# Score and value matmuls of a sliding-window attention, issued alternately between two halves of the array

## The chip, the cores and the metric

The kernel runs on one core of a Trainium2 chip, in one launch. The metric is the device time of that launch in microseconds (us), as the median of several runs. PE is the matmul engine, PEld its weight load, DVE, ACT and POOL are the vector, scalar and GpSimd engines, SP is the queue that issues most DMAs.

## The reference, cut to what matters

The program is one inference step of a one-layer hybrid decoder: LayerNorm and adaLN modulation, a combined input projection, a Mamba-2 group and a sliding-window attention group side by side, an output projection, and a squared-ReLU MLP. 2048 prompt tokens and 32 sample tokens go through it. The change touches the prompt's attention alone:

```python
WINDOW = 128; HEAD_DIM = 64; N_Q = 8; N_KV = 2; Q_PER_KV = 4
...
s = jnp.einsum('bnqgrd,bnkgd->bngrqk', qb, kk) * (HEAD_DIM ** -0.5)
s = jnp.where(mask[None, :, None, None], s, -jnp.inf)
p = sink_softmax(s, sinks.astype(jnp.float32).reshape(N_KV, Q_PER_KV)[:, :, None, None])
o = jnp.einsum('bngrqk,bnkgd->bnqgrd', p, vv)
```

A block of 128 queries looks at the keys of its own block and of the one before. A head has 64 elements, so a score contracts over 64 rows, and the values of one key-value head give 64 output columns.

## The kernel before, in words

The work goes through the chip in stages. **Sweep 1** (the functions named `st_...`) takes 16 prompt tiles of 128 tokens and one tile of sample tokens, and makes for each the modulated input, the projection to dt, q, k and v ("slab": `st_slab`, 24 matmuls for each of two halves), and the whole attention. Sweep 2 makes the Mamba group (`xproj`, `zproj`, `ssd1`, `ssd2`), and after it come the output projection and the MLP. Sweep 1 ends some 400 us after the start of the span; the MLP takes most of the rest.

In sweep 1 the loop over `i` handles several tiles at once, each at another step: slab 0 of tile i, `st_PT` of tile i-2, `st_score` of tile i-1, slab 1 of tile i, one step of the adaLN weights (`ada_mm`, L257, four column strips of 32; eight such steps in all), `st_PV` of tile i-2, `st_qkT` of tile i, and the transposes of a later tile's input (L320).

- `st_qkT` (L395) transposes q (L406) and a doubled k (L410: each key head stands twice, in partitions 0 to 63 and 64 to 127). ACT rounds the results to the type fp32r (`qh`, `kTh`), DVE keeps the remainders (`ql`, `kTl`).
- `st_score` (L414) makes the scores of a tile. For each key-value head `g` and each parity `par` of the query head it takes one PSUM buffer and writes two score blocks into it, each by `mm3` (L164): high by high (L165), high by low (L166), low by high (L167). That is 4 buffers and 24 matmuls a tile. `par` chooses the partitions, 0 to 63 or 64 to 127, and by that the rows of the array. ACT (L433) and DVE (L434) copy the buffers out into `S`, and `softmax` (L378) follows: a maximum on DVE, eight exponentials on ACT (L389), a scaling on POOL (L393).
- `st_PT` (L438) transposes the probabilities (L449). `st_PV` (L456) multiplies them with the values: for each of one or two terms, and each `g`, one matmul with 64 output columns at column 0 or 64 of the array (L461), all in plain float32. ACT copies the result to `ao` (L464) and stores it.

The PSUM buffers come from three rings: `mm` with 3 buffers, `tr` with 2, `sc` with 3. A buffer is taken again when its last reader is done.

The order of the instructions on each engine is not the order of the code. The framework's scheduler sorts them, engine by engine, when the program is built, by a model of its own of how long each takes; only what depends on each other, and what is pinned by hand, keeps its order. On the chip each engine then works through its list and waits where a semaphore isn't there yet.

Of the kernel before, what the change touches and what calls it, by code (L numbers as in the profile page):

```python
# [118 lines left out]
def body(tc, I, O):  # L119
    nc = tc.nc  # L120
    V, S, G, PE, D = nc.vector, nc.scalar, nc.gpsimd, nc.tensor, nc.sync
# [14 lines left out]
    def sc_tile():  # L136
        return ps.tile([128, 512], F32, tag="sc", name="sc", bufs=3)
# [18 lines left out]

    def sum2(out, tmp, w):
        PE.matmul(out[:ND, :w], lhsT=idt[:2 * ND, 192:224], rhs=tmp[:2 * ND, :w], start=True, stop=True)

    def split(hi, lo, src, eng=None):  # L160
        S.activation(hi, src, AF.Copy)  # L161
        (eng or V).tensor_tensor(lo, src, hi.bitcast(F32), ALU.subtract)  # L162

    def mm3(out, ahi, alo, bhi, blo, first=True, last=True):  # L164
        PE.matmul(out, lhsT=ahi, rhs=bhi, start=first, stop=False)  # L165
        PE.matmul(out, lhsT=ahi, rhs=blo, start=False, stop=False)  # L166
        PE.matmul(out, lhsT=alo, rhs=bhi, start=False, stop=last)  # L167
# [63 lines left out]
    start = ExitStack()  # L231
# [66 lines left out]
    kTh = p1.tile([128, 2, 3, 128], F32R, name="kTh")  # L298
    kTl = p1.tile([128, 2, 3, 128], F32R, name="kTl")
# [46 lines left out]
    def st_slab(t, n):  # L346
# [8 lines left out]
        if t == NTILE:  # L355
            tmp = mm_dec(p1.tile([128, 512], F32, tag="ao", name="tmp", bufs=2), 388, lambda k: hh[:, 0, k, :2 * ND],
                         lambda k, l: (W1l if l else W1h)[k][:, sl])
            sum2(mm, tmp, 388)
        elif t > 2:
            for k in range(8):  # L360
                mm3(mm[:P, :388], hh[:, 0, k, :P], hh[:, 1, k, :P], W1h[k][:, sl], W1l[k][:, sl], k == 0, k == 7)
# [16 lines left out]
    def softmax(p, Sx, P, nh, nk, sink):  # L378
        mx = p.tile([128, 8], F32, tag="mx", name="mx", bufs=2)
        nm = p.tile([128, 8], F32, tag="nm", name="nm", bufs=2)  # L380
        su = p.tile([128, 8], F32, tag="su", name="su", bufs=2)
        ex = p.tile([128, 8], F32, tag="ex", name="ex", bufs=2)
        V.tensor_reduce(mx[:P, :nh], Sx, AX.X, ALU.max)
        V.scalar_tensor_tensor(mx[:P, :nh], mx[:P, :nh], 0.125, sink, ALU.mult, ALU.max)
        V.tensor_scalar(nm[:P, :nh], mx[:P, :nh], -1.0, None, ALU.mult)
        V.tensor_tensor(ex[:P, :nh], sink, mx[:P, :nh], ALU.subtract)
        S.activation(ex[:P, :nh], ex[:P, :nh], AF.Exp)
        for h in range(nh):
            S.activation(Sx[:, h, :], Sx[:, h, :], AF.Exp, bias=nm[:P, h:h + 1], scale=0.125,  # L389
                         accum_out=su[:P, h:h + 1])  # L390
        V.tensor_tensor(su[:P, :nh], su[:P, :nh], ex[:P, :nh], ALU.add)
        V.reciprocal(su[:P, :nh], su[:P, :nh])
        G.tensor_tensor(Sx, Sx, su[:P, :nh].unsqueeze(2).to_broadcast([P, nh, nk]), ALU.mult)  # L393
# [20 lines left out]
    def st_score(t):  # L414
        qh, ql = tl.pop(("q", t))
        if t == 0:
            slots, nk, ci = slice(0, 1), 1, 0
        else:
            slots, nk, ci = [(slice(0, 3, 2), 2, 0), (slice(0, 2), 2, 1), (slice(1, 3), 2, 1)][t % 3]
        ge = cc(C_GE, 128).bitcast(U32).unsqueeze(1).to_broadcast([128, 2, 128])  # L420
        Sx = p1.tile([128, 8, 128], F32, tag="S", name="S", bufs=2)
        if t == 0:
            V.memset(Sx, NEG)
        for g in range(2):
            for par in range(2):
                sc = sc_tile().rearrange("p (j s n) -> p j s n", j=2, s=2)
                rp = slice(64 * par, 64 * par + 64)
                for jj in range(2):
                    q2 = 2 * g + jj
                    mm3(sc[:, jj, 0:nk, :], qh[rp, q2, :], ql[rp, q2, :], kTh[rp, g, slots, :], kTl[rp, g, slots, :])  # L430
                hs = slice(4 * g + 2 * par, 4 * g + 2 * par + 2)
                if t > 0:
                    S.activation(Sx[:, hs, :], sc[:, :, 1 - ci, :], AF.Copy)  # L433
                V.copy_predicated(Sx[:, hs, :], ge, sc[:, :, ci, :])  # L434
        softmax(p1, Sx, 128, 8, 128, sm[:, 3, :])
        tl["S", t] = Sx
# [19 lines left out]
    def st_PV(t):  # L456
        terms = tl.pop(("PT", t))
        o = sc_tile()
        for i, (vv, pt) in enumerate(terms):
            for g in range(2):  # L460
                PE.matmul(o[64 * g:64 * g + 64, :], lhsT=vv[:, 64 * g:64 * g + 64], rhs=pt[:, g, :],  # L461
                          start=i == 0, stop=i == len(terms) - 1, tile_position=(0, 64 * g))
        ao = p1.tile([128, 4, 128], F32, tag="ao", name="ao", bufs=2)
        S.activation(ao.rearrange("p r n -> p (r n)"), o, AF.Copy)  # L464
        S.dma_start(out=att_d[t], in_=ao)
# [219 lines left out]
    n = len(seq)  # L685
# [66 lines left out]
    for i in range(n + 3):  # L752
        if i == 10:
            start.close()
        g = lambda j: seq[j] if 0 <= j < n else None
# [11 lines left out]
        if g(i - 1) is not None and g(i - 1) < NTILE:  # L767
            st_score(g(i - 1))
# [4 lines left out]
        if g(i - 2) is not None and g(i - 2) < NTILE:  # L773
            st_PV(g(i - 2))
# [568 lines left out]
    def dec_steps():  # L1343
# [12 lines left out]
        for n in range(2):  # L1356
            sum2(pp[n], b[:, 512 * n:512 * n + 512], 512)
# [166 lines left out]
```

## Time and profile before

| | |
|---|---|
| median of 3 runs | 2519.69 us (2519.55 to 2523.37) |
| profiled execution, its own time | 2522.31 us |
| its span, first to last instruction | 2520.5 us |
| granted clock of the matmul engine, mean | 0.985 |
| DVE busy | 1510.5 us (60%) |
| ACT busy | 720.2 us (29%) |
| POOL busy | 930.8 us (37%) |

Two views carry the prediction. One gives the busy time of each engine in stretches of the span. The other lists the instructions of one engine in order of time: start in us, how long the row lasts, engine, line, operation, out<-in, shapes, how many instructions in a row were merged ("x2"), and in brackets what an idle engine waited for. A float32 matmul whose operands aren't of type fp32r stands there as two records. The records of matmuls overlap, so what one costs is read from the starts, not from the lengths.

### The profile page before, as it was taken

What the parts mean: (1) busy time and instruction counts of PE and PEld (TensorE: products, weight loads), DVE (VectorE), ACT (ScalarE), POOL (GpSimd) and SP (SyncE); (2) the same over time, 40 slices, a digit from 0 to 9 for tenths busy, and PEclk for the clock granted to TensorE, in tenths of its full rate; (3) what the DMA queues carried; (4) which work ended last, traced back from release to release, by engine and by line L of the source; (5) the groups of instructions that cost most, each with busy time, mean ns of one, the idle gap of its engine ahead of it and who ended that gap; (6) DMA issues with size and microseconds to landing.
All of it is one profiled execution on the core that took longest, in us unless ns stands there. A gap on an engine that the chain in (4) does not pass through costs nothing.

```text
span 2520.5 us, 32205 instructions
## 1 busy us (share of the span) xinstructions
PE 2421.1 (96%) x12694; PEld 2004.7 (80%) x12694; DVE 1510.5 (60%) x2582; ACT 720.2 (29%) x1434; POOL 930.8 (37%) x602
## 2 busy tenths in 40 slices
PE   7899999999998988899999999999999999999997
PEld 6567787977997766787888888887788988988985
DVE  6756666977788988744434444447844344344347
ACT  3544465333342222222121211213221221221221
POOL 4323431233223544633243333426532332332335
PEclk9999999999999999899999999999999999999998
DMA  8644333223335336411111211118211111111111
GB/s 318 255 173 160 118 124 91 73 72 109 98 115 174 117 127 221 162 59 58 48 59 42 63 51 39 53 43 238 100 51 34 43 59 34 43 59 34 43 46 70
DMA packets 116504, 244.19 MB, mean 97 GB/s; under 512 B 25984, under 2 KB 61248, under 8 KB 113200
## 3 DMA queue, kind: packets, MB, share of 16 engines
q1 hardware_dynamic: 111952, 232.15, 27.6%
q10 hardware_dynamic: 4400, 9.98, 1.1%
q8 instruction: 100, 1.64, 0.3%
q14 instruction: 52, 0.43, 0.1%
HBM read 187.74 MB, written 55.37 MB: 96 GB/s over the span
## 4 chain that ended last, share of the span: by engine, by line
PE 53%; DVE 3%; POOL 1%; issue 1%; DMA 0%; ACT 0%; SPq 0%; POOLq 0%; DVEq 0%; ACTq 0%
PE sc L165 10%; PE sc L167 10%; PE sc L166 10%; PE mm L165 5%; PE mm L167 5%; PE mm L166 5%; PE tr L165 2%; PE tr L167 2%; PE tr L166 2%; PE tr L1276 1%; DVE p L1231 1%; DVE nb L1300 0%; DVE p L1232 0%; POOL rs L173 0%; DVE p L1307 0%
## 5 line engine op out<-in xcount | busy, mean ns | idle before, releaser
L162 POOL TENSOR_TENSOR wdl<-st,wdh 128x1024 fp32r<-128x1024 f32 x63 | 164.1, 2605 | 531.4 <-ACT wdh L161 531.4
L1261 DVE TENSOR_TENSOR r<-r 128x320 f32<-128x320 f32 (+1 forms) x160 | 151.3, 946 | 299.0 <-ACT u L1257 101.6
L1288 DVE TENSOR_TENSOR p<-mm,p 128x512 f32<-128x512 f32 x298 | 202.7, 687 | 176.6 <-PE mm L167 176.6
L161 ACT ACTIVATE wdh<-st 128x1024 fp32r<-128x1024 f32 x63 | 66.8, 1061 | 628.4 <-PE mm L167 245.4
L165 PE MATMUL sc<-H,wvh 128*128 128x352 f32 (+1 forms) x640 | 227.1, 355 | 5.3 <-ACT r L1255 5.3
L167 PE MATMUL sc<-H,wvl 128*128 128x352 f32 (+1 forms) x640 | 226.1, 353 | 0.0
L166 PE MATMUL sc<-H,wvh 128*128 128x352 f32 (+1 forms) x640 | 225.9, 353 | 0.0
L165 PE MATMUL sc<-H,wuh 128*128 128x352 f32 (+1 forms) x640 | 224.4, 351 | 0.0
L167 PE MATMUL sc<-H,wul 128*128 128x352 f32 (+1 forms) x640 | 223.9, 350 | 0.0
L166 PE MATMUL sc<-H,wuh 128*128 128x352 f32 (+1 forms) x640 | 223.6, 349 | 0.0
L1255 ACT ACTIVATE r<-sc 128x352 f32<-128x352 f32 (+1 forms) x160 | 81.7, 511 | 271.6 <-PE sc L167 230.9
L165 PEld LDWEIGHTS sc<-H,wvh 128*128 128x128 f32 x640 | 120.8, 189 | 18.3 <-ACT r L1255 5.7
L166 PEld LDWEIGHTS sc<-H,wvh 128*128 128x128 f32 x640 | 120.7, 189 | 12.0
L167 PEld LDWEIGHTS sc<-H,wvl 128*128 128x128 f32 x640 | 120.4, 188 | 12.1
L165 PEld LDWEIGHTS sc<-H,wuh 128*128 128x128 f32 x640 | 120.4, 188 | 11.4 <-ACT r L1255 0.8
L167 PEld LDWEIGHTS sc<-H,wul 128*128 128x128 f32 x640 | 120.8, 189 | 10.5
L166 PEld LDWEIGHTS sc<-H,wuh 128*128 128x128 f32 x640 | 120.7, 189 | 10.2
L1137 DVE TENSOR_TENSOR st<-st,gf 128x1024 f32<-128x1024 f32 x64 | 83.8, 1309 | 55.6 <-POOL wdl L162 46.3
L1288 DVE TENSOR_TENSOR p<-tr,p 128x512 f32<-128x512 f32 x102 | 69.9, 687 | 74.8 <-PE tr L167 74.8
L173 POOL TENSOR_TENSOR rs<-ve,mhalf 128x1 f32<-128x1 f32 (+2 forms) x68 | 49.1, 722 | 174.9 <-DVE ve L172 158.1
L1260 DVE TENSOR_TENSOR ud<-r 128x32 f32<-128x32 f32 x32 | 56.5, 1766 | 94.4 <-ACT r L1255 94.4
L652 DVE SCALAR_TENSOR_TENSOR xc<-xq,cvw,xc 128x256 f32<-128x256 f32 x192 | 102.0, 535 | 2.7
(485 smaller groups left out, 6630.8 us busy)
## 6 DMA issues: line engine op xcount, KB each, us to landing
st<-in_wd SPq DMA_DIRECT2D x64, 512.0 KB
st<-in_wu SPq DMA_DIRECT2D x63, 512.0 KB
wa<-in_w_ada SPq DMA_DIRECT2D x32, 512.0 KB
hT_d<-hb SPq DMA_DIRECT2D x16, 1024.0 KB
hT<-hT_d SPq DMA_DIRECT2D x16, 512.0 KB
hT<-hT_d SPq DMA_DIRECT2D x8, 1024.0 KB
csb<-cs_d SPq DMA_DIRECT2D x16, 512.0 KB
p<-xhat_d SPq DMA_DIRECT2D x16, 512.0 KB
```

The lines of the kernel that those rows point to most:

```text
L161: S.activation(hi, src, AF.Copy)
L162: (eng or V).tensor_tensor(lo, src, hi.bitcast(F32), ALU.subtract)
L165: PE.matmul(out, lhsT=ahi, rhs=bhi, start=first, stop=False)
L166: PE.matmul(out, lhsT=ahi, rhs=blo, start=False, stop=False)
L167: PE.matmul(out, lhsT=alo, rhs=bhi, start=False, stop=last)
L173: G.tensor_tensor(r[:P], v[:P], mhalf[:P, 0:n], ALU.pow)
L652: V.scalar_tensor_tensor(dst_, src(j), cvw[:, f, j:j + 1], dst_, ALU.mult, ALU.add)
L1137: V.tensor_tensor(st, raw, scale, ALU.mult)
L1255: S.activation(r[:, :n], mm[:, :n], AF.Relu)
L1260: V.tensor_tensor(ud, r[:, w:n], r[:, w:n], ALU.mult)
L1261: V.tensor_tensor(r[:, :w], r[:, :w], r[:, :w], ALU.mult)
L1288: V.tensor_tensor(acc[t][:, sl], mm, acc[t][:, sl], ALU.add)
```

## The change

A helper, `side_by_side`, calls a list of functions that each issue a matmul, and ties each instruction to the one before it by an edge without a semaphore: the scheduler must keep them in this order, and the chip waits for nothing. It may still put other instructions between them.

`st_score` now opens the buffers of both parities of a `g` first and issues their matmuls in turn, parity 1 and then parity 0. The fourth buffer of a tile (`g` = 1, `par` = 1) comes from the `mm` ring. `st_PV` puts its matmuls in the same chain, `g` = 1 before `g` = 0. The copies, the softmax and all other code stay as they were.

```diff
+    def side_by_side(calls):
+        prev = None
+        for fn in calls:
+            ins = fn()
+            if prev is not None:
+                tc.add_manual_dep(ins.ins, prev.ins.name,
+                                  mybir.DependencyInfo(mybir.DependencyClass.NoSync, mybir.DependencyReason.DATA),
+                                  reason="side_by_side")
+            prev = ins
...
+        rp = lambda par: slice(64 * par, 64 * par + 64)
         for g in range(2):
+            scs = [(sc_tile, mm_tile)[g * par]().rearrange("p (j s n) -> p j s n", j=2, s=2) for par in range(2)]
+            side_by_side([lambda jj=jj, i=i, par=par: PE.matmul(
+                scs[par][:, jj, 0:nk, :], lhsT=(ql if i == 2 else qh)[rp(par), 2 * g + jj, :],
+                rhs=(kTl if i == 1 else kTh)[rp(par), g, slots, :], start=i == 0, stop=i == 2)
+                for jj in range(2) for i in range(3) for par in (1, 0)])
             for par in range(2):
-                sc = sc_tile().rearrange("p (j s n) -> p j s n", j=2, s=2)
-                rp = slice(64 * par, 64 * par + 64)
-                for jj in range(2):
-                    q2 = 2 * g + jj
-                    mm3(sc[:, jj, 0:nk, :], qh[rp, q2, :], ql[rp, q2, :], kTh[rp, g, slots, :], kTl[rp, g, slots, :])
+                sc = scs[par]
...
-        for i, (vv, pt) in enumerate(terms):
-            for g in range(2):
-                PE.matmul(o[64 * g:64 * g + 64, :], lhsT=vv[:, 64 * g:64 * g + 64], rhs=pt[:, g, :],
-                          start=i == 0, stop=i == len(terms) - 1, tile_position=(0, 64 * g))
+        side_by_side([lambda i=i, vv=vv, pt=pt, g=g: PE.matmul(
+            o[64 * g:64 * g + 64, :], lhsT=vv[:, 64 * g:64 * g + 64], rhs=pt[:, g, :], start=i == 0,
+            stop=i == len(terms) - 1, tile_position=(0, 64 * g))
+            for i, (vv, pt) in enumerate(terms) for g in (1, 0)])
```

Since the scheduler sorts anew, everything in sweep 1 moves a little; from early in sweep 2 on the lists of all engines are the same. PE has 12117 matmuls before and after. In the changed program the lines of the old code stand ten to twelve higher: L437 is a score matmul, L471 a value matmul, L416 and L420 are the transposes of q and k, L267 is an adaLN matmul.

The first place is on PE, the scores of tile 7, where the numbers tell the PSUM buffers apart. Before, `sc_2207` and `sc_2225` belong to parity 0 and `sc_2216` to parity 1:

```order
L165 MATMUL sc_2207<-kTh_139,qh_2113 128x256
L166 MATMUL sc_2207<-kTl_140,qh_2113 128x256
L167 MATMUL sc_2207<-kTh_139,ql_2114 128x256
L165 MATMUL sc_2207<-kTh_139,qh_2113 128x256
L166 MATMUL sc_2207<-kTl_140,qh_2113 128x256
L167 MATMUL sc_2207<-kTh_139,ql_2114 128x256
L165 MATMUL sc_2216<-kTh_139,qh_2113 128x256
L166 MATMUL sc_2216<-kTl_140,qh_2113 128x256
L167 MATMUL sc_2216<-kTh_139,ql_2114 128x256
L165 MATMUL sc_2216<-kTh_139,qh_2113 128x256
L166 MATMUL sc_2216<-kTl_140,qh_2113 128x256
L167 MATMUL sc_2216<-kTh_139,ql_2114 128x256
```

After it, at the same tile, `sc_2208` is parity 1 and `sc_2207` parity 0 of the first head; `mm_2226` is the fourth buffer:

```order
L437 MATMUL sc_2208<-kTh_139,ql_2114 128x256
L437 MATMUL sc_2207<-kTh_139,ql_2114 128x256
L437 MATMUL sc_2208<-kTh_139,qh_2113 128x256
L437 MATMUL sc_2207<-kTh_139,qh_2113 128x256
L437 MATMUL sc_2208<-kTl_140,qh_2113 128x256
L437 MATMUL sc_2207<-kTl_140,qh_2113 128x256
L437 MATMUL sc_2208<-kTh_139,ql_2114 128x256
L437 MATMUL sc_2207<-kTh_139,ql_2114 128x256
L437 MATMUL mm_2226<-kTl_140,qh_2113 128x256
L437 MATMUL sc_2225<-kTl_140,qh_2113 128x256
L437 MATMUL mm_2226<-kTh_139,ql_2114 128x256
L437 MATMUL sc_2225<-kTh_139,ql_2114 128x256
```

Six matmuls of one parity in a row became a strict alternation, and the fourth buffer's six, which stood in a run of their own 20 rows later, have joined the others.

The second place is on PE too, the value matmuls of one tile. Before, the two matmuls of a term (`PT_1749`) are apart, with four transposes between them; "x2" is one matmul for each column half:

```order
L257 MATMUL mm_1858<-wa_1660,scT_109 32x512
L461 MATMUL sc_1883<-PT_1749,v_1064 64x512
L406 MATMUL tr_1895<-idt_74,qkv_1720 128x128 x4
L461 MATMUL sc_1883<-PT_1749,v_1064 64x512
L461 MATMUL sc_1883<-PC_1750,vd_1751 64x512 x2
L410 MATMUL tr_1902<-idt_74,kd_1891 128x128 x2
```

And with the change:

```order
L267 MATMUL mm_1858<-wa_1658,scT_109 32x512 x2
L267 MATMUL mm_1858<-wa_1660,scT_109 32x512 x2
L471 MATMUL sc_1883<-PT_1749,v_1064 64x512 x2
L471 MATMUL sc_1883<-PC_1750,vd_1751 64x512 x2
L272 MATMUL mm_1869<-part_1867,idt_74 9x512
```

Here the halves stand together, and the adaLN matmuls ahead of them are not broken up any more.

The third place is on PE at the last tile, where the scheduler puts the first four scores of a tile (one for each buffer, high by high) ahead of the rest. Before, 29 rows of `xproj` matmuls stand between the transposes of k (L410) and the first score; the first of them:

```order
L461 MATMUL sc_3829<-PC_3722,vd_3723 64x512
L410 MATMUL tr_3850<-idt_74,kd_3839 128x128 x2
L166 MATMUL mm_4235<-hT2_3856,pg0_3981 128x256
L167 MATMUL mm_4235<-hT2_3855,pg1_3982 128x256
L165 MATMUL mm_4235<-hT2_3855,pg2_3985 128x256
```

And with the change:

```order
L471 MATMUL sc_3829<-PC_3722,vd_3723 64x512 x2
L416 MATMUL tr_3843<-idt_74,qkv_3692 128x128 x4
L420 MATMUL tr_3850<-idt_74,kd_3839 128x128 x2
L437 MATMUL sc_3918<-kTh_139,qh_3841 128x256
L437 MATMUL sc_3917<-kTh_139,qh_3841 128x256
L437 MATMUL mm_3936<-kTh_139,qh_3841 128x256
L437 MATMUL sc_3935<-kTh_139,qh_3841 128x256
L175 MATMUL mm_3999<-hT2_3855,Wx00_3683 128x256
```

The scores that need the copies of these very transposes now follow them at once. The same holds at tiles 0, 1, 8 and 10 to 14, with none or one to three rows between.

On ACT, at the same last tile and with the change, the copies `qh` and `kTh` (L171) stand behind the eight exponentials of the tile before (L399):

```order
L399 ACTIVATE S,su<-S,nm 128x128
L397 ACTIVATE ex<-ex 128x8
L399 ACTIVATE S,su<-S,nm 128x128 x7
L171 ACTIVATE qh<-tr 128x512
L171 ACTIVATE kTh<-tr 128x2x128
L171 ACTIVATE pg_4133<-wzst 128x512
```

Before, the order of these three is the same, but PE had other work in between.

## The prediction

> **What bounds the kernel now.** I read the page first: its busy times and the first line of its chain of waits.
>
> ```profile
> PE 2421.1 (96%) x12694; PEld 2004.7 (80%) x12694; DVE 1510.5 (60%) x2582; ACT 720.2 (29%) x1434; POOL 930.8 (37%) x602
> PE 53%; DVE 3%; POOL 1%; issue 1%; DMA 0%; ACT 0%; SPq 0%; POOLq 0%; DVEq 0%; ACTq 0%
> ```
>
> PE is the engine on which the end waits. But the change works in sweep 1 alone, so the second view is the busy time by stretch, from 100 us to the end of sweep 1. Columns: PE, PEld, DVE, ACT, POOL, then the granted clock.
>
> ```profile
> 100.00:200.00 100.00, 100.00 (x571) 66.76 (x564) 58.82 (x148) 47.09 (x156) 27.52 (x26) 1.00 0.51 177
> 200.00:300.00 100.00, 100.00 (x602) 77.79 (x601) 64.40 (x178) 44.13 (x140) 37.60 (x30) 1.00 0.34 117
> 300.00:320.00 20.00, 13.88 (x69) 8.86 (x67) 13.73 (x19) 8.61 (x16) 11.26 (x6) 0.74 0.76 240
> 340.00:360.00 20.00, 19.53 (x137) 16.84 (x134) 17.80 (x26) 14.05 (x28) 13.12 (x7) 1.00 0.39 139
> 380.00:400.00 20.00, 14.56 (x89) 9.80 (x88) 15.49 (x51) 14.90 (x41) 1.90 (x1) 0.83 0.04 14
> ```
>
> From 100 to 300 us PE has no idle time at all, and no other engine is above 65%. There a us of PE work that goes is a us of the kernel. From 300 us on PE idles now and then; the waits of PE between 60 and 450 us say for whom (total us, times, longest):
>
> ```profile
> PE sc L165 <- DVE S L434: 9.3, 3, 6.1
> PE mm L568 <- DVE dkw L559: 3.0, 1, 3.0
> ```
>
> The 9.3 us are scores that wait until DVE has emptied a score buffer: a tile needs four, the ring has three.
>
> **The change, part by part.** No matmul, copy or DMA is added or removed; what changes is how PE's matmuls lie beside each other. The third view, PE in order of time between 200 and 230 us, prices that.
>
> ```profile
> 200.60 1.03 PE L320 MATMUL tr<-idt,xb 128*128 128x128 f32 x8
> 201.56 0.38 PE L165 MATMUL sc<-kTh,qh 64*128 64x256 f32 x1
> 201.78 0.28 PE L166 MATMUL sc<-kTl,qh 64*128 64x256 f32 x1
> 201.90 0.28 PE L167 MATMUL sc<-kTh,ql 64*128 64x256 f32 x1
> 201.91 0.39 PE L165 MATMUL sc<-kTh,qh 64*128 64x256 f32 x2
> 202.13 0.28 PE L166 MATMUL sc<-kTl,qh 64*128 64x256 f32 x2
> ...
> 202.97 0.28 PE L167 MATMUL sc<-kTh,ql 64*128 64x256 f32 x1
> 203.17 0.44 PE L166 MATMUL mm<-pg,hb 128*128 128x388 f32 x1
> ...
> 206.72 1.90 PE L257 MATMUL mm<-wa,scT 128*32 128x512 f32 x10
> 208.55 0.38 PE L165 MATMUL sc<-kTh,qh 64*128 64x256 f32 x1
> ...
> 209.46 1.06 PE L257 MATMUL mm<-wa,scT 128*32 128x512 f32 x6
> 210.45 1.08 PE L461 MATMUL sc<-PT,v 128*64 128x512 f32 x4
> 211.36 1.03 PE L461 MATMUL sc<-PC,vd 128*64 128x512 f32 x4
> 212.31 0.66 PE L406 MATMUL tr<-idt,qkv 128*128 128x128 f32 x4
> ...
> 217.49 0.50 PE L165 MATMUL sc<-kTh,qh 64*128 64x256 f32 x3
> 217.92 0.84 PE L158 MATMUL mm<-tmp,idt 64*32 64x388 f32 x2
> ...
> 228.64 1.07 PE L461 MATMUL sc<-PT,v 128*64 128x512 f32 x2
> 229.64 0.55 PE L320 MATMUL tr<-idt,x 128*128 128x128 f32 x3
> ```
>
> *Scores.* A score starts 0.12 us after the one before it in the same rows of the array (201.78 and 201.90). Two of different parity start together: the rows "x2" hold one of each. This already happens without the change: the list has six of parity 0, six of parity 1, six of parity 0, and these 18 take 203.17 - 201.56 = 1.61 us, that is 12 slots of 0.116 and 0.2 for going into and out of the narrow shape. The other six of the tile stand alone: 208.55 to 209.46, 0.91 us, six slots and 0.2. The three at 217.49 (parities 0, 1, 0) take 0.43: two slots and 0.2. So a run costs 0.2 + 0.116 per slot, and a tile has 18 slots now and 12 when all pair up. That is 6 x 0.116 x 15 = 10.4 us, and some 0.4 for tile 0, whose matmuls are half as wide. The lists have 48 runs of scores before and 36 with the change: 12 x 0.2 = 2.4 us. Together 13.2 us.
>
> [...]
>
> *Values.* Four records, one matmul for each column half, take 210.45 to 211.36; two such pairs in a row 1.86 us; one matmul alone 228.64 to 229.64 = 1.00 us. So a slot costs 0.87 us, holding one half or both, and a run 0.13 more. Of 31 pairs, 8 cost a slot too many in the list of before (as `PT_1749` above: half alone, then three); with the change all 31 stand together. 8 x 0.87 = 7.0, and 30 runs become 22, 8 x 0.13 = 1.0. Together 8.0 us.
>
> *adaLN matmuls, a side effect.* Eight in one piece take 1.85 us:
>
> ```profile
> 188.99 1.92 PE L257 MATMUL mm<-wa,scT 128*32 128x512 f32 x16
> 190.84 1.08 PE L461 MATMUL sc<-PT,v 128*64 128x512 f32 x4
> ```
>
> Broken by six scores they take 1.83 (206.72 to 208.55) and 0.99 (209.46 to 210.45): 0.97 us more for one more piece. The eight steps lie in 16 pieces before, in 10 after: 6 x 0.97 = 5.8 us.
>
> *Neighbours.* The eight transposes ahead of 201.56 take 0.96 us, about 0.09 more than 8 x 0.109, the step between transposes inside such a row (0.66 us for the four at 212.31 holds three steps and one full length). Runs of the three narrow kinds fall from 94 to 68: 26 x 0.09 = 2.3 us.
>
> PE's work falls by 13.2 + 8.0 + 5.8 + 2.3 = **29.3 us**.
>
> *A wait that goes.* The fourth score buffer comes from the `mm` ring now, so the 9.3 us of waits for L434 go. If DVE is late all the same, the next user of the ring waits; the value lies between 0 and 9.3, and I take 9.3, since the first scores are now issued 3 us and more ahead of most others.
>
> *A wait that comes.* At tiles 0, 1, 8 and 10 to 15 the first scores stand right behind the transposes that feed them. How long the copies take, from the same execution:
>
> ```profile
> 297.08 0.66 PE L406 MATMUL tr<-idt,qkv 128*128 128x128 f32 x4
> 297.83 0.60 ACT L161 ACTIVATE qh<-tr 128x512 fp32r<-128x512 f32 x1 [0.92 <-PE tr L406]
> ...
> 298.92 0.44 PE L410 MATMUL tr<-idt,kd 128*128 128x128 f32 x2
> 299.39 0.39 ACT L161 ACTIVATE kTh<-tr 128x256 fp32r<-128x256 f32 x1 [0.95 <-PE tr L410]
> ```
>
> From L410 to the end of `kTh` 0.86 us pass, of which PE's own two transposes fill 0.2. So at least 0.65 us a tile, 9 x 0.65 = 6 us in all. The other end comes from what stands before these copies on ACT: eight exponentials, and before those DVE's work on the scores (counts, busy us, mean ns):
>
> ```profile
> L389 ACT ACTIVATE S<-S,nm 128x128 f32<-128x128 f32 x128 | 49.6, 390 | 21.1 <-DVE nm L385 21.1
> L434 DVE COPY_PREDICATED S<-c,sc 128x256 f32<-128x256 uint32 x64 | 26.2, 440 | 12.5 <-ACT S L433 12.5
> L389 ACT ACTIVATION_READ_ACCUMULATOR S<-S,nm 128x1 f32 x128 | 24.2, 189 | 0.0
> L383 DVE TENSOR_REDUCE mx<-S 128x8 f32<-128x1024 f32 x16 | 19.5, 1217 | 0.3
> ```
>
> After the last score: 4 x 0.44 + 1.22 + about 1 of small work on DVE, then 8 x (0.39 + 0.19) = 4.6 on ACT, then up to 0.6 (`ao`) + 0.5 (`qkv`) + 0.60 + 0.39: some 10 to 12 us until `kTh` is there. In PE's list some 7 to 9 us of work stand between at tiles 10 to 14, and 3 us at tile 15. That is 1 to 5 us each for five tiles, and up to 9 for the last. At the upper end 5 x 4 + 9 + 2 = 31 us. I take 2 us for tiles 10 to 14, 5 for the last, 2 for the other three: 17 us, nearer the middle, since ACT idles about half of this time now. Behind a waiting score stand the next tile's slab on PE, and behind that everything.
>
> *Nothing else.* POOL (607 instructions) and SP (537) keep theirs, a few rows swap places; ACT loads its tables ten times less (1.28 us each) at the end of sweep 1, where ACT is not the bound; I count nothing.
>
> **Sum.** -29.3 - 9.3 + 17 = -21.6 us. The profiled execution took 2522.31 (span 2520.5 and 1.8 around it), so 2500.7; the median of the runs stands 2.6 lower, and the forecast for a median is 2519.69 - 21.6 = **2498 us**.
>
> **The rivals.**
> *The copies become the bound* (2511). The new waits come out at the upper end, and the 9.3 come back elsewhere: -29.3 + 31 - some 10 for what doesn't add = about -8. For it: the rows of tiles 10 to 15 above. Against: DVE at 64% and ACT at 44% from 200 to 300 us. [...]
> *No new waits* (2484). Only the 6 us at the lower end: -29.3 - 9.3 + 6 = -32.6, and up to 3 more from clock that is not lost (0.74 around the wait at 306 us).
> *The pairs don't form* (2510). If strict alternation went one by one, only values and adaLN would gain: -8.0 - 5.8 + the waits. Against: the three at 217.49 alternate and took two slots.
> *Slower: the `mm` ring* (2545). A score holds one of three `mm` buffers from the first four scores until the copies; slab and adaLN accumulators have two left. If each of two slabs a tile waited 1.5 us behind the exponentials on ACT, 32 x 1.5 = 48 - 21.6 = +26. It decides from 0.7 us a slab. Against: in the list only two slabs follow within 2 us of the score that held their buffer.
>
> **How the numbers follow.** Forecast (2490 to 2506) 0.5; no new waits 0.17; copies as the bound 0.2; no pairs 0.06; slower 0.07. Two in ten may be left out: the slow rival and part of both tails, so the range is 2482 to 2513. A measurement of this kernel tells about 0.2%, 5 us, from no change. Faster by more than that: 0.5 + 0.17 + most of 0.2 and 0.06 = 0.87; within it 0.07; slower 0.06.
>
> **What would show it.** The scores of a tile in 12 starts instead of 18, one run of 20 in about 1.4 us; no value matmul alone, 0.87 us a pair; L257 in 10 pieces; no wait of a score for L434, but waits of a score for ACT's `kTh` at the nine tiles. It would be wrong if slabs wait for ACT's copies of `mm` buffers, if PE's idle time from 200 to 400 us grows by over 30 us, or if the paired starts fall apart.

## The result, and the profile after

| | before | after |
|---|---|---|
| median | 2521.53 us (4 runs) | 2507.18 us (4 runs) |
| profiled execution, its own time | 2522.31 us | 2506.52 us |
| its span | 2520.5 us | 2504.7 us |
| mean granted clock | 0.985 | 0.984 |

The ratio is 0.9941, with a 95% interval of 0.9926 to 0.9956: 14.4 us faster. The kernel was run again later on, beside other runs of the kernel before, and gave 2506.66 us and 0.9946 (0.9933 to 0.9958).

The busy times on the page of the changed kernel, and under them the stretches that were shown of before (columns as there):

```profile
PE 2396.3 (96%) x12694; PEld 1996.7 (80%) x12694; DVE 1501.9 (60%) x2582; ACT 705.1 (28%) x1424; POOL 930.2 (37%) x602
```

```profile
100.00:200.00 100.00, 96.59 (x630) 68.37 (x628) 63.94 (x165) 48.72 (x164) 34.85 (x31) 1.00 0.52 184
200.00:300.00 100.00, 93.31 (x576) 72.23 (x572) 65.34 (x176) 51.25 (x163) 44.06 (x31) 0.98 0.44 148
300.00:320.00 20.00, 19.26 (x115) 15.87 (x114) 9.02 (x23) 9.02 (x31) 6.68 (x6) 0.93 0.49 156
340.00:360.00 20.00, 12.54 (x90) 10.03 (x88) 15.11 (x34) 13.36 (x41) 8.76 (x6) 0.83 0.39 128
380.00:400.00 20.00, 20.00 (x122) 16.68 (x121) 12.56 (x46) 8.98 (x20) 2.09 (x2) 1.00 0.30 102
```

PE lost 24.8 us of busy time over the kernel, but the kernel only 15.8 in these two executions: between 100 and 300 us PE was never idle before, and now is for 10 us. The waits of PE between 60 and 430 us name what it is idle for (total, times, longest):

```profile
PE sc L437 <- ACT kTh L171: 13.0, 9, 4.9
PE tr L330 <- DVE mv L190: 5.6, 1, 5.6
PE tr L416 <- DVE qkv L386: 3.5, 2, 2.5
PE sc L471 <- DVE S L446: 2.8, 1, 2.8
PE mm L272 <- ACT part L270: 2.0, 1, 2.0
```

The waits of scores for DVE's copies (L434 before) are gone; nine first scores wait for `kTh`. PE in order of time shows the pairs. These are 20 of the 24 scores of a tile; "x2" is one score of each parity:

```profile
212.16 0.39 PE L437 MATMUL sc<-kTl,qh 64*128 64x256 f32 x2
212.38 0.28 PE L437 MATMUL sc<-kTh,ql 64*128 64x256 f32 x2
212.50 0.28 PE L437 MATMUL sc<-kTh,qh 64*128 64x256 f32 x2
...
213.34 0.28 PE L437 MATMUL mm<-kTh,ql 64*128 64x256 f32 x1
213.34 0.28 PE L437 MATMUL sc<-kTh,ql 64*128 64x256 f32 x1
213.55 0.39 PE L153 MATMUL mm<-pg,hb 128*64 128x388 f32 x1
```

Ten starts, 0.12 us apart, 1.39 us in all. The values now always stand with both halves together, 0.9 us a pair:

```profile
200.32 1.08 PE L471 MATMUL sc<-PT,v 128*64 128x512 f32 x4
201.23 1.03 PE L471 MATMUL sc<-PC,vd 128*64 128x512 f32 x4
```

**A better yardstick than the total.** All these programs hold the same 12694 matmul records, and the 3000th starts in sweep 2, at 520.5 us before. From there to the 4700th (780 us) the two executions run in step: the lead of the changed kernel is 18.2 us at the 3000th and 18.2 at the 4700th. In the output projection, from 780 to 1030 us, where PE waits for DVE, POOL and inputs on their way, the lead goes down to about 13 and comes out at 15.8; with most other kernels below it goes up there. So I compare kernels by the start of the 3000th record as well, and split it into the time that PE had no matmul running (idle) and the rest (work), counted over the PE records from the 300th, which starts at 54.3 to 54.7 us in all.

| kernel | median us | ratio to before (95%) | 3000th at | idle | work |
|---|---|---|---|---|---|
| before | 2521.53 | | 520.5 | 21.2 | 444.8 |
| the change | 2507.18 | 0.9941 (0.9926 to 0.9956) | 502.3 | 32.7 | 415.2 |
| again | 2506.66 | 0.9946 (0.9933 to 0.9958) | 501.7 | 31.9 | 415.3 |
| scores_only | 2512.82 | 0.9968 (0.9956 to 0.9980) | 509.9 | 32.6 | 423.0 |
| values_only | 2513.41 | 0.9965 (0.9954 to 0.9977) | 508.7 | 21.9 | 432.2 |
| sc4 | 2510.38 | 0.9962 (0.9948 to 0.9976) | 509.1 | 29.7 | 425.1 |
| mm4 | 2511.47 | 0.9962 (0.9949 to 0.9975) | 507.4 | 27.9 | 425.3 |
| parity01 | 2515.15 | 0.9977 (0.9968 to 0.9985) | 511.2 | 32.2 | 424.6 |
| remfirst | 2521.02 | 0.9996 (0.9986 to 1.0006) | 517.4 | 42.0 | 421.0 |
| halves | 2542.33 | 1.0082 (1.0066 to 1.0098) | 539.6 | 38.1 | 447.2 |
| dvecopies | 2510.33 | 0.9955 (0.9940 to 0.9969) | 507.2 | 29.8 | 423.1 |
| dvecopies_rem | 2528.71 | 1.0024 (1.0013 to 1.0034) | 525.9 | 49.1 | 422.4 |
| swap | 2493.48 | 0.9893 (0.9878 to 0.9908) | 493.2 | 22.9 | 416.0 |
| swap_rem | 2493.81 | 0.9892 (0.9879 to 0.9906) | 493.2 | 23.8 | 414.6 |

The change took 29.6 us of work off PE and put 11.5 us of idle time in.

### The profile page after: what moved, and what is told of

The parts are those of the page before. It is cut to its first block, busy times and chain, and to the rows that moved or that the text cites. A ratio compares the mean times of both kernels' runs of the same rounds, so it can differ in the third digit from the quotient of the medians.

```text
span 2504.7 us, 32204 instructions
## 1 busy us (share of the span) xinstructions
PE 2396.3 (96%) x12694; PEld 1996.7 (80%) x12694; DVE 1501.9 (60%) x2582; ACT 705.1 (28%) x1424; POOL 930.2 (37%) x602
## 4 chain that ended last, share of the span: by engine, by line
PE 54%; DVE 3%; POOL 1%; issue 1%; DMA 0%; SPq 0%; ACT 0%; POOLq 0%; DVEq 0%; ACTq 0%
PE sc L175 11%; PE sc L177 10%; PE sc L176 10%; PE mm L175 5%; PE mm L177 5%; PE mm L176 5%; PE tr L177 2%; PE tr L175 2%; PE tr L176 2%; PE tr L1288 1%; DVE p L1243 1%; DVE nb L1312 0%; DVE p L1244 0%; POOL rs L183 0%; DVE p L1319 0%
## 5 line engine op out<-in xcount | busy, mean ns | idle before, releaser
L171 ACT ACTIVATE wdh<-st 128x1024 fp32r<-128x1024 f32 x63 | 66.8, 1061 | 629.0 <-PE mm L177 244.8
L175 PEld LDWEIGHTS sc<-H,wvh 128*128 128x128 f32 x640 | 120.8, 189 | 18.2 <-ACT r L1267 5.6
```

## The experiments

### The parts of the change

**scores_only**: the change, with the value matmuls in the old form.

```diff
-        side_by_side([lambda i=i, vv=vv, pt=pt, g=g: PE.matmul(
-            o[64 * g:64 * g + 64, :], ...
-            for i, (vv, pt) in enumerate(terms) for g in (1, 0)])
+        for i, (vv, pt) in enumerate(terms):
+            for g in range(2):
+                PE.matmul(o[64 * g:64 * g + 64, :], ...
```

> Only the scores alternate (with the fourth buffer from the mm ring); the value matmuls are issued as before. Theory (the terms add: PE time per slot and run, plus waits): the list has 28 runs of value matmuls with 8 extra slots, against 22 runs and none with the whole change, 8 x 0.87 + 6 x 0.13 = +7.8 us, and 32 runs of scores against 36, 4 x 0.3 = -1.2. The first scores stand as close behind the transposes of k as with the whole change (0 to 4 rows at tiles 9 to 15), so the waits for kTh stay near 13 us. 2507.2 + 6.6 = 2514 us, 7.7 us faster than before. Rival (the scores carry the gain, values lie beside waits anyway): within 2 us of the whole change, 2505 to 2509.

Measured 2512.82 us, 5.6 more than the change (7.6 at the 3000th record). The value matmuls take 39.0 us of PE without waits instead of 30.5, idle time is the same. Work is up by 7.8 us, about the theory's 7.8 - 1.2: on top of the scores the values' term adds.

**values_only**: the kernel before, with only `st_PV` in the new form (the diff above, reversed).

> Only the value matmuls are chained; scores and their buffers as before. Theory (the terms add): values -9.6 us as the trace of the whole change shows it, four pieces of adaLN matmuls fewer (4 x 0.97 = -3.9), four runs of scores fewer (-1.2), no more pairs of scores; first scores stand 11 rows and more behind the transposes of k but at tile 11, so the waits stay like before, at most 5 us more. 2521.5 - 14.7 + 0 to 5: 2507 to 2512, I say 2509. Rival (the gain needs the alternation of the scores): 2515 or more.

Measured 2513.41, just outside the theory's range, and 1.6 us below the rival's. At the 3000th record the gain is 11.8 us: 12.6 us of work less, 0.7 more idle. Idle time stays the same in sum, though not in kind: waits of scores for score buffers fall from 9.3 to 3.5 us, and others come in their place. The values alone bring most of the work that the theory adds up, with no score alternating.

**sc4**: the change, with all four score buffers from the `sc` ring of three.

```diff
-            scs = [(sc_tile, mm_tile)[g * par]().rearrange("p (j s n) -> p j s n", j=2, s=2) for par in range(2)]
+            scs = [sc_tile().rearrange("p (j s n) -> p j s n", j=2, s=2) for par in range(2)]
```

> The whole change, but the fourth score buffer comes from the ring of three score buffers as before. Theory (the terms add): 44 runs of scores instead of 36 (+2.4 us), five more pieces of adaLN matmuls (+4.9), three more runs of values (+0.4); no first score stands within 14 rows of the transposes of k after tile 1, so the 13 us of waits for kTh go, and waits for the copies of the score buffers come back, 9.3 us as before. 2507.2 + 7.7 - 13 + 9.3 = 2511 us. Rival (four buffers are what makes the alternation pay; with three the second pair of every tile waits for the copies, some 1.5 us a tile, 24 us in all): 2525 us or more.

Measured 2510.38; the theory said 2511. The two first waits of PE in this kernel:

```profile
PE sc L437 <- DVE S L446: 11.7, 5, 6.8
PE sc L437 <- ACT kTh L171: 3.9, 2, 3.3
```

The waits for the score buffers are back (9.3 before), and those for `kTh` fall from 13.0 to 3.9. The alternation does not need the fourth buffer.

**mm4**: the kernel before, with only the fourth buffer from the `mm` ring.

```diff
-                sc = sc_tile().rearrange("p (j s n) -> p j s n", j=2, s=2)
+                sc = (sc_tile, mm_tile)[g * par]().rearrange("p (j s n) -> p j s n", j=2, s=2)
```

> The kernel before with only the fourth score buffer taken from the mm ring; no matmul is chained. The list then has runs of 5 scores of one parity, 5 of the other, 5, 5. Theory (a score starts beside up to some four earlier ones of the other parity that have not started, so such a run of 20 takes about 12 slots, against 10 in strict alternation): some 230 slots against 297 before, 67 x 0.116 = -7.8 us; ten runs of scores fewer (-3.0), seven pieces of adaLN matmuls fewer (-6.8), one more slot of values (+0.9); waits for score buffers go (-9.3) and waits for kTh come as with the whole change (+13). 2521.5 - 13 = 2508.5 us, that is about as fast as the whole change although nothing alternates. Rival (scores pair only where the list alternates): a run of 20 takes 20 slots, some 350 in all, +6.2 instead of -7.8: 2522 us.

Measured 2511.47; three us above the theory, ten below the rival. Nothing alternates in this kernel: its list has five scores of one parity, five of the other, five, five. PE in order of time:

```profile
135.09 0.38 PE L166 MATMUL sc<-kTl,qh 64*128 64x256 f32 x1
135.32 0.28 PE L167 MATMUL sc<-kTh,ql 64*128 64x256 f32 x1
135.32 0.38 PE L166 MATMUL sc<-kTl,qh 64*128 64x256 f32 x1
...
136.50 0.28 PE L167 MATMUL mm<-kTh,ql 64*128 64x256 f32 x1
136.71 0.44 PE L165 MATMUL mm<-pg,hb 128*128 128x388 f32 x1
```

The row of 0.38 us at 135.32 is the sixth of the list and starts with the second. Four places were there in the trace of before too: of the 18 scores from 201.56 us on, the seventh starts at 201.91, beside the third at 201.90. The 20 of mm4 take 12 starts and 1.61 us, against 10 and 1.39 alternating. For such a run the alternation itself is therefore worth 0.22 us. From this kernel to scores_only the scores' time on PE falls from 35.2 to 29.8 us in all, part of it because there are 32 runs instead of 38; but idle time rises by 4.7 and the median does not fall (2511.47, 2512.82).

**parity01**: the change, each chain begun with the other half.

```diff
-                for jj in range(2) for i in range(3) for par in (1, 0)])
+                for jj in range(2) for i in range(3) for par in (0, 1)])
...
-            for i, (vv, pt) in enumerate(terms) for g in (1, 0)])
+            for i, (vv, pt) in enumerate(terms) for g in (0, 1)])
```

> The whole change, but both chains begin with the other half: parity 0 then 1, column half 0 then 1. The list then has the value matmuls apart again (28 runs, 8 extra slots) and all else as in the run with the scores alone. Theory (what keeps the column halves together is that the half whose operand is ready last is asked for first; the alternation by itself does nothing for them): like the scores alone, 2512 to 2514 us, 3000th matmul at 510 us. Rival (an edge in the list is worth its gain whatever the order): 2505 to 2509.

Measured 2515.15 and 511.2: like the scores alone, and 1 us above the expected interval. The values take 40.2 us, as before the change (40.1). So the edge alone is worth nothing for the values. The probabilities of `g` = 0 are copied out first; begun with that half, the scheduler sends it off alone, begun with `g` = 1 both are ready. That the readiness is the reason is read from the lists, not tried apart.

**again**: the change, unchanged.

> The whole change once more, unchanged. Theory (sweep 1 and sweep 2 repeat to a few tenths of a us, and what differs between executions arises in the output projection after 760 us): the 3000th matmul starts at 502.3 us as in the first profile, within 0.5 us; the median lies between 2505 and 2509. Rival (sweep 1 itself varies by some us, so the differences between the kernels at this point are partly chance): off by more than 1 us there.

The 3000th record starts at 501.65, 0.65 us earlier: a little more than expected, well under the rival. Differences of a us or less at this point are not told apart; those used here are larger.

### How far ahead of its place in the list a score starts

**remfirst**: the change, with the product by `kTl` first in each block, so that no score can be sent ahead.

```diff
-                rhs=(kTl if i == 1 else kTh)[rp(par), g, slots, :], start=i == 0, stop=i == 2)
-                for jj in range(2) for i in range(3) for par in (1, 0)])
+                rhs=(kTl if i == 1 else kTh)[rp(par), g, slots, :], start=i == 1, stop=i == 0)
+                for jj in range(2) for i in (1, 2, 0) for par in (1, 0)])
```

> The whole change, but in each score block the product with kTl comes first (kTl by qh, kTh by ql, kTh by qh), so the first score of a tile needs the last of the copies and the scheduler can't send four scores ahead. The list then has 27 runs of scores against 36, most of all 24 in one piece, 14 rows behind the transposes of k at most tiles and 8 at the last ones. Theory (the scores sent ahead are what waits for kTh, 13 us, and they cost a run of their own): nine runs fewer -2.7 us, two pieces of adaLN fewer -1.9, two runs of values fewer -0.3; the waits for kTh fall from 13 to some 6 us of waits for kTl and for the probabilities that now stand ahead of the scores at the last tiles. 2507.2 - 4.9 - 7 = 2495 to 2502, I say 2499. Rival (a tile at the end of the sweep is bound by the chain scores, copies, softmax, transposes, and the waits only move to another row): 2503 to 2508.

**halves**: the same, with all four buffers opened first and all 24 scores in one chain, twelve of parity 1 and then twelve of parity 0. The line that changes the order:

```diff
-                for jj in range(2) for i in (1, 2, 0) for par in (1, 0)])
+            for par in (1, 0) for g in range(2) for jj in range(2) for i in (1, 2, 0)])
```

> Like the run with the kTl product first, and almost the same list, but the 24 scores of a tile are chained as 12 of parity 1 and then 12 of parity 0. Theory (a score can start beside three to four earlier ones of the other parity that are still queued, and no further): 12 + 12 less 3 = 21 slots a tile instead of 12, 16 x 9 x 0.116 = +16 us against that run, and pairs in the trace only where the halves meet. Rival one (the array's row groups have queues as deep as needed): 12 to 13 slots, within 2 us of that run. [...]

I take halves first. PE in order of time; parity 1 starts at 80.95, parity 0 with the row of 0.38 us at 82.02:

```profile
80.95 0.39 PE L437 MATMUL sc<-kTl,qh 64*128 64x256 f32 x1 [1.22 <-DVE kTl L172]
81.18 0.28 PE L437 MATMUL sc<-kTh,ql 64*128 64x256 f32 x1
...
82.02 0.28 PE L437 MATMUL mm<-kTh,qh 64*128 64x256 f32 x1
82.02 0.38 PE L437 MATMUL sc<-kTl,qh 64*128 64x256 f32 x1
...
83.43 0.28 PE L437 MATMUL sc<-kTh,qh 64*128 64x256 f32 x1
83.64 0.64 PE L267 MATMUL mm<-wa,scT 128*32 128x512 f32 x4
```

The thirteenth score of the list starts beside the ninth, past the three that stand between them; the run has 21 starts and takes 2.69 us, against 12 and 1.62 in remfirst. So a score does start ahead of its place in the list, and here by four places and no more: mm4 has the same four, the sixth beside the second. In a tile that starts at 136.96 us, where the granted clock was 0.50, it is the ninth again (138.84 beside 138.83 us). One start after another, with one shared where the halves meet or none, would have made 23 or 24 starts and, by the sum of the theory, 20 to 22 us more. The time, 21.3 us above remfirst, fits that better than the theory's 16, but the starts do not (21). The scores' time on PE rises from 37.8 to 58.1 us; 16 x 9 x 0.116 = 16.7 of these 20.3 are the starts, and the rest goes with the lower clock in a number of tiles, below (the mean clock from 60 to 400 us is 0.88 here and 0.93 in remfirst).

Remfirst itself was a miss: 2521 instead of 2499, above the rival's 2503 to 2508 too, and no gain at all on before. Work did not fall (421.0 us against 415.2 with the change) and idle time rose to 42.0. The first wait of PE there, and the place where it is longest, PE and then DVE in order of time:

```profile
PE tr L330 <- DVE ql L172: 16.8, 7, 3.4
```

```profile
158.78 1.51 PE L330 MATMUL tr<-idt,hbuf 128*128 128x128 f32 x8 [3.40 <-DVE ql L172]
160.22 0.58 PE L437 MATMUL sc<-kTl,qh 64*128 64x256 f32 x2
...
161.03 0.41 PE L437 MATMUL sc<-kTl,qh 64*128 64x256 f32 x2
161.24 0.41 PE L437 MATMUL sc<-kTh,ql 64*128 64x256 f32 x2
```

```profile
156.85 1.29 DVE L189 BATCH_NORM_STATS2 bst<-xb 128x6 f32<-128x512 f32 x2 [4.57 <-DMA xb<-in_x]
158.05 0.68 DVE L172 TENSOR_TENSOR ql<-tr,qh 128x512 fp32r<-128x512 f32 x1
158.64 0.41 DVE L172 TENSOR_TENSOR kTl<-tr,kTh 128x256 fp32r<-128x256 f32 x1
```

The transposes of the next input need a `tr` buffer; it is held until `ql` is taken from it; `ql` is ready to run at about 155 us, but stands on DVE behind the statistics of an input that arrives at 156.85. With the change, PE has slab matmuls at such places and only needs ACT's `kTh`. So the rival was right that the waits would move, though not by the chain that I named for it: it was the `tr` ring, and DVE's queue.

The rows show a second cost. Scores that start 0.12 us apart elsewhere start 0.21 us apart here. The same kernel's stretches around it, granted clock in the third column from the end:

```profile
150.00:158.00 8.00, 5.38 (x31) 4.81 (x30) 3.39 (x7) 1.37 (x3) 0.91 (x1) 1.00 0.66 209
160.20:163.00 2.80, 2.80 (x25) 2.65 (x25) 2.20 (x5) 1.10 (x4) 2.50 (x2) 0.55 0.37 151
163.00:170.00 7.00, 7.00 (x46) 5.61 (x49) 3.71 (x9) 4.56 (x19) 2.53 (x2) 1.00 0.00 0
```

After the wait of 3.40 us the granted clock is 0.55 from 160.2 to 163.0 us, and these scores are 1.1 us longer (2.72 instead of 1.61). Elsewhere in the same kernel a shorter wait is followed by the same: PE waits 2.1 us from 92.4 us on, and has a clock of 0.50 while it works again.

```profile
92.40:94.40 2.00, 0.00 (x0) 0.00 (x0) 1.07 (x3) 1.21 (x4) 1.82 (x1) 1.00 1.09 415
94.50:97.80 3.30, 3.27 (x20) 2.94 (x22) 1.66 (x4) 1.22 (x3) 0.00 (x0) 0.50 1.00 415
```

Seven of the runs of twelve starts are lengthened so in remfirst, behind waits of 1.3 to 3.4 us, and no long run with the change. Other waits of up to 2.0 us, as the one from 162.5 us on with the change, left the clock at 1.00; what decides in between is not shown.

### Where the first scores wait

**dvecopies**: the change, with the copies `qh` and `kTh` on DVE.

```diff
-        split(qh, ql, tr)
+        V.tensor_copy(qh, tr)
+        V.tensor_tensor(ql, tr, qh.bitcast(F32), ALU.subtract)
...
-        split(kTh[:, :, t % 3, :], kTl[:, :, t % 3, :], tr[:, 0:2, :])
+        V.tensor_copy(kTh[:, :, t % 3, :], tr[:, 0:2, :])
+        V.tensor_tensor(kTl[:, :, t % 3, :], tr[:, 0:2, :], kTh[:, :, t % 3, :].bitcast(F32), ALU.subtract)
```

> The whole change, and the copies qh and kTh (rounding q and k to fp32r) go to DVE instead of ACT; the remainders stay on DVE. Theory (the first scores wait for kTh because the eight exponentials stand ahead of the copies on ACT): the waits of scores for the copies, 13 us, fall to about 7, no single one over 2.5 us, since DVE is idle at the long ones; four runs of scores more, +1.2. 2507.2 - 6 + 1 = 2502 us. Rival (the copies just queue on DVE, which has 65% of the time taken): waits of 13 us or more, 2507 to 2512.

Why I expected it: ACT at the longest wait with the change, 4.9 us from 345.6 to 350.4:

```profile
345.84 0.63 ACT L171 ACTIVATE pg<-wzst 128x512 fp32r<-128x512 f32 x1 [2.26 <-DMA wzst<-in_wz]
346.38 0.39 ACT L399 ACTIVATE S<-S,nm 128x128 f32<-128x128 f32 x1
...
349.55 0.57 ACT L171 ACTIVATE qh<-tr 128x512 fp32r<-128x512 f32 x1
350.03 0.36 ACT L171 ACTIVATE kTh<-tr 128x256 fp32r<-128x256 f32 x1
```

ACT first waits for a weight on its way, then does eight exponentials of the tile before, and only then the copies. On DVE they wait for none of that:

```profile
PE sc L439 <- DVE kTh L422: 10.7, 9, 1.9
```

The longest is 1.9 us now, as the theory has it, but the sum only fell from 13.0 to 10.7. With the copies on ACT, two of the nine waits are long, 4.9 and 3.7 us, both behind eight exponentials, and the other seven have 0.6 us each on average; on DVE all nine have 1.2. What queues in front makes two long waits out of nine; the short distance makes all nine. The median, 2510.33, misses the theory's 2502 and is no better than that of the change. The waits explain only part of that: PE's work rose by 7.9 us, where I had counted 1, in scores, values and adaLN matmuls (5.3 us together) and elsewhere. Why is not shown.

**dvecopies_rem**: both edits.

> Both: the product with kTl first, and the copies qh and kTh on DVE. Theory: the list is that of the run with the kTl product first but for two more runs of scores (+0.6 us); the scores stand 8 to 14 rows, 1.4 us and more, behind the transposes of k, which covers most of the copies now that no exponentials are ahead of them: waits of scores for copies 3 us or less, against some 6. 2496 us. Rival (the chain of a tile at the end of the sweep bounds): no faster than the run with the kTl product first alone.

A larger miss than remfirst: 2528.71 instead of 2496, with 49.1 us idle. It is no faster than remfirst, as the rival said, but again not by the rival's chain: the longest waits are those of transposes for `tr` buffers held for `ql` (18.2 us in seven) and those of scores for `kTl` (10.5 in three). That more work on DVE ahead of the remainders makes them later still is how I read it; it was not tried apart.

**swap**: the change, with the second slab of a tile written ahead of the scores of the tile before it.

```diff
-        if g(i - 1) is not None and g(i - 1) < NTILE:
-            st_score(g(i - 1))
         if t is not None:
             st_slab(t, 1)
+        if g(i - 1) is not None and g(i - 1) < NTILE:
+            st_score(g(i - 1))
```

> The whole change, and in the loop the second slab of a tile is written ahead of the scores of the tile before it. The list has 33 runs of scores against 36 and two pieces of adaLN fewer, -2.7 us; the first scores stand 50 to 69 rows behind the transposes of k at tiles 2 to 7, 8 and 20 at tiles 13 and 14, still none at 11, 12 and 15. Theory (waits are set by that distance): waits for kTh 13 to 11 us, nothing new elsewhere: 2503 us. Rival (with scores later in the tile the softmax ends later, and the transposes of the probabilities or the rows behind remainders on DVE wait instead): 2508 to 2520.

**2493.48 us**, ratio 0.9893: the fastest kernel here, 13.7 us below the change and 28 below before. At the 3000th record 9.1 of the 13.7 us are there, and they are not the work, which is the same (416.0 and 415.2), but the idle time: 22.9 us instead of 32.7. The other 4.6 us come behind sweep 1, most of them in the output projection, and I have no cause for them. Its first waits:

```profile
PE sc L437 <- ACT kTh L171: 6.6, 7, 2.4
PE sc L471 <- ACT pg L171: 6.3, 1, 6.3
PE tr L330 <- DVE mv L190: 4.5, 1, 4.5
```

The forecast was 2503; the direction was right, the size was not, since I counted on pieces of adaLN and runs of scores (2.7 us), which don't show in the sum of the work, and on only 2 us of waits.

**swap_rem**: the swap with the product by `kTl` first.

> The same swap with the kTl product first in each block. The list has 27 runs of scores, first scores 39 to 69 rows behind the transposes of k at tiles 2 to 8, 8 to 41 at tiles 9 to 14. Theory (the run with the kTl product first lost because the scores and the transposes of the next input stood 8 to 14 rows behind, too close for DVE's remainders, which queue behind the statistics of an input still on its way): with more rows between the waits for ql and kTl fall from 25 us to 8 or less, 2502 to 2508. Rival (the remainders are late whatever stands between): 2515 or more.

2493.81, with 3.5 us of waits of transposes for `ql` where remfirst had 16.8, and 4.6 for `kTl`. That agrees with the theory that with more rows of PE's list between the transposes and what needs the remainders, the late remainders cost little; the time is 8 us below its interval.

## Why the prediction came out as it did

The range held the time: 2507.2, in 2482 to 2513; the forecast of 2498 was 9 us too low, and a gain of 21.6 was forecast where 14.4 to 15.2 were measured. The mechanism was right, less work on PE against new waits for `kTh`; its sizes were right in part by luck. By its steps, from the two traces:

- *Scores, 13.2 us.* Time on PE without waits 46.0 before and 31.5 after, 14.5 less; 36 runs, as forecast. A tile takes 12 starts.
- *Values, 8.0.* 40.1 and 30.5: 9.6 less. No half stands alone.
- *adaLN matmuls, 5.8.* 22.6 us in 16 pieces and 17.5 in 10: 5.1 less.
- *Neighbours, 2.3.* The three terms above make 29.2 us, so 0.4 is left of the work that went.
- *PE's work in all, 29.3.* 444.8 and 415.2: **29.6** less. That this half of the sum was right to 1% is luck: scores and values brought 2.9 us more than forecast, adaLN matmuls and neighbours 2.6 less.
- *The wait that goes, 9.3.* No score waits for a score buffer any more; 2.8 us come back at one value matmul, which takes its buffer from the same ring (L471 behind L446).
- *The wait that comes, 17.* **13.0**, at nine tiles, the number that the list gave. At the last tile 4.9 (forecast 5), at tiles 10 to 14 0.4, 0.5, 3.7, 0.7 and 0.8, in all 6.1 where I took 10.
- *Nothing else.* This is the step that failed. PE is idle 11.5 us more than before, not 17 - 9.3 = 7.7. Beside the two waits of the sum, 13.0 - 9.3 = 3.7, that is 7.8 us net where I had counted none: transposes of an input wait 5.6 us for its LayerNorm (L190), where it was 3.5 before, q's transposes 3.5 for the rotation of q and k (L386), an adaLN sum 2.0, the value matmul 2.8. Only because the waits for `kTh` came out 4.0 us below forecast did the idle time miss by 3.8 us and not by 7.8; that is luck too. Less work alone does not bring such waits: scores_only has as much idle time with 21.8 us less work (32.6), swap has 22.9 with 28.8 less. That points to the order of the list; it was not tried apart. At the 3000th record the gain was 18.2 us.
- From there to the end 2.4 us more are missing in these two executions, 3.8 by the medians. From the 3000th to the 6000th record the lead changes by something between 2.4 us less (the change) and 2.3 more (values_only: 11.8 and 14.1); in three executions (again, parity01, swap_rem) sweep 2 had taken 1.6 to 2.0 already. The change itself, executed again, lost 0.7 over the same records, so I don't read a cause into that. And the base of the forecast, a median of 2519.69 us, came out at 2521.5 to 2522.2 in the later runs.

Of the rivals, the copies as the bound was right in kind (PE now reaches the copies before they are done), but it put the new waits at 31 us; no new waits put them at 6. No slab waits for an `mm` buffer that a score holds. Pairs form (a tile takes 12 starts), and form without the change (18 scores in 12 starts before). One price of the prediction was off here: if strict alternation went one by one, the scores would also lose the pairs that they had before, 6 slots a tile, which that rival left out.

What the prediction did not see is which part does it. The fourth buffer alone brings 10 us, the values alone 9, the scores with the buffer 9, all but the buffer 10 to 12, and the whole 14 to 15; the first four are not told apart by their intervals. On PE's work the terms add only roughly (the values take off 12.6 us alone and 7.8 on top of the scores), and in mm4, sc4, scores_only and the change 6.7 to 11.5 us of new idle time pay part of it back. In both comparisons that add the alternation of scores, the time does not fall clearly. From mm4 to scores_only 2.3 us of work go and 4.7 of idle time come; from values_only to sc4 it is 7.1 and 7.8, with the 3000th record at 508.7 and 509.1 and medians of 2513.41 and 2510.38.

Not tried: the fourth buffer and the values together without the alternation, which may do as well as the whole; the swap without the change, so how much of its 28 us needs the alternation is open; and a kernel that keeps the list of the change row for row and puts only the first scores later.

## What to carry to other kernels

Price a reordering in two sums, the work that goes from the bounding engine and the rows that then stand between a producer and its consumer; the larger terms of the first could be had to 10 to 20% here from starts in the trace, and the second decides how much of it is kept. Where two small matmuls can share the array, let the list bring them within four places of each other, as far apart as they still started together here; strict alternation adds little to that (0.22 us for a run of 20 scores, 10 starts instead of 12). In a chain of edges, try beginning with the operand that is ready last: begun with the other, the scheduler sent the first one off alone here (40.2 us for the values instead of 30.5).

## What the runs showed of the hardware

- A matmul of the other rows of the array starts beside one that stands up to four places before it in the list (before: the seventh score with the third, 201.91 and 201.90 us; mm4: the sixth with the second, 135.32; halves: the thirteenth with the ninth, 82.02, and again at a granted clock of 0.50, 138.84 and 138.83). In halves none starts further ahead.
- A wait of PE can cost more than itself: in remfirst the granted clock was 0.55 for 2.8 us behind one of 3.4 us, with scores 0.21 instead of 0.12 us apart, and 0.50 for 3.3 us behind one of 2.1 us; with the change it was 1.00 behind one of 2.0 us.
- In ten of thirteen executions sweep 2 kept its distance from before to 0.3 us from the 3000th to the 4000th record (520 to 675 us), and in three it lost 1.6 to 2.0; up to the 6000th record the lead changed by up to 2.4 us either way. A start in the trace, taken right behind the stage that was changed, repeated to 0.65 us in the one kernel that was traced twice, while the totals of one kernel's runs spread over 4 to 13 us.
